# RWKV-7 branch of a hybrid block on one Trainium2 core: token-major tiles by identity products of array parts, in a task of their own, and U and V in a tile per pair

## The chip, the core and the metric

The kernel runs on one core of one Trainium2 chip. A core has five engines that are used here: TensorE (PE, with its weight loads shown as PEld), VectorE (DVE), ScalarE (ACT), GpSimd (POOL) and SyncE (SP), which issues nearly all transfers. Each engine runs its own instructions in their order and waits on semaphores for the others. The metric is the device time of one execution in microseconds. The kernel before takes 2975.77 us, the median of three runs (2969.96 to 2988.65).

## What is computed

A block of two layers maps a latent stream of 256 tokens and a context of 256 tokens, 1024 channels wide, to the latent stream. In each layer a normed input goes through one wide projection into three branches, which are gated and summed, and then through a gated feed-forward part (FFN):

```
p  = rms_norm(x) modulated @ w_in            # columns: mLSTM | RG-LRU | RWKV-7 ("rw") | merge gates
y  = sig(g_ml)*(mlstm(p) @ out_ml) + sig(g_lru)*(rglru(p) @ out_lru) + sig(g_rw)*(rwkv7(p) @ out_rw)
x += gate1 * (y @ w_out);   x += gate2 * swiglu(rms_norm(x) modulated)

# rwkv7, 16 heads of 64, forward and backward over context, then over the latent tokens
kap = k*k_k / norm(k*k_k);  w = exp(-c*sigmoid(decay));  a = sigmoid(iclr);  kt = k*(1+(a-1)*k_a)
def step(S, (r, w, k, v, kap, kapa)):        # per head, state S is 64 x 64
    S = S*w - (S@kap) kapa^T + v k^T
    return S, S@r
out = (layernorm(y)*ln_w + ln_b + sum(r*(kt_f+kt_b)*r_k)*v) * gate
```

## The kernel before

Arrays lie with channels on the partitions and tokens along the free axis. Products in full precision are made of three reduced ones (a high and a low part of weights and input), so a weight block goes from DMA to a cast on ACT (`whi`), a subtraction on DVE (`wlo`) and three matmuls on PE.

The change lies in the RWKV part, which the kernel works out in chunks of 32 tokens. Its work comes in **units**, u = 0 to 7: four groups of two pairs of heads, each once for the context (even u) and once for the latent tokens (odd u). A unit goes through these functions:

- `rw_prep`: the norm of k (from L783), decay and rate from low-rank products (`low`, `wtanh`, `decay`), the scaled arrays (`rows`), and then `chunks` (L759 to 780): products of all 8 chunks of a direction into two PSUM banks of the tag `sm`, masked by DVE into `Am` (L772), and sent to memory for the solve (L778). Behind that stands the **token stage** (L829 to 888): POOL scales `bks` (L830), and k-side and v-side tiles must be brought from channel-major to token-major form, as weights and inputs of the chain. `tokens` (L848) transposes four blocks of 128x128 into one PSUM bank (L852). `quads` (L840) copies the four quarters of that bank to their places with four copies (L845), those of the forward direction on ACT, those of the backward one on DVE. Four banks give `bkT`. Two give `UV`, after two ACT copies that order v by chunk (L876). Between them stands the product for the bonus term `bv` (L869).
- `rw_solve`: 30 pairs of POOL instructions (L930, L932) invert a small triangular system per chunk. Its input N comes from memory (L924), its result goes to memory (L937) and back into `Am` (L942), all on SP's queue.
- `rw_chain`: eight steps, one after the other, for the eight chunks of both directions. In each, PE adds the state's part into `xy`, DVE copies it to `xs` (L1001) and scales the state (L1005), PE multiplies it by the solved `Am` into one PSUM tile `u2`, four copies bring that to `UV` (j=1 on ACT, L1028; j=0 on DVE, L1031), PE makes the state's update and the output, and DVE writes the new state `Sn` (L1046, L1048) and the output (L1058, L1060).
- `rw_tail`: layer norm over the head, a transposing product and the gate.

`rw_prep` runs for the eight units one after the other in one task, `rw_chain` in another. Both, the loads (`rw_load`) and the gate product (`rw_gate`) stand beside the **fills** (`products`): the projections of all branches, 1776 matmuls per layer (L258, tile `mm`). `weave` (L296) sets the order when the program is built: it goes through the tasks in their order in a list, the fills last. A task yields what it waits for: an estimated time (`at`, `on`), an event of another task (`until`), or a lock. A task that can go on is preferred, and a fill is put in whenever PE has lately had fewer than 4800 columns of work in a stretch of estimated time. So every edit of costs or tasks changes where the fills stand.

Behind this stretch stand `ml_gates`, and then `ml_head` and `lru` for four groups (the mLSTM and RG-LRU branches). `gates()` makes the merge-gate products (576 matmuls per layer, L415, loaded by SP in pieces of 512 KB), of which some are put between the heads, and the rest behind them. Then comes the merge (L1486), the output projection and the FFN (L415). The compiler's scheduler orders these sections, and may move their instructions up into the RWKV stretch where that has room.

## Time and profile before

| | kernel before |
| --- | --- |
| median of three runs | 2975.77 us (2969.96 to 2988.65) |
| the profiled execution | 2990.54 us, span 2988.8 us |
| PE busy | 2663.0 us, 89% |
| PEld busy | 2037.4 us, 68% |
| DVE busy | 1877.0 us, 63% |
| ACT busy | 1260.8 us, 42% |
| POOL busy | 794.4 us, 27% |
| mean granted clock of PE | 0.953 |

The profile is one execution, so its times stand against its own 2990.54 us and not against the median. Busy shares are means over stages with different limits. The table alone says that PE is busy for most of the span. The waits of a stage say what an engine stood still for, and the chain of waits is followed back from the last instruction.

### The profile page before, as it was taken

The numbers are of one execution on the slowest core, as the hardware profiler recorded it, in microseconds if no ns is written. First come the engines' busy times: TensorE is split into PE (matmuls) and PEld (weight loads), VectorE is DVE, ScalarE is ACT, GpSimd is POOL, SyncE is SP. The second block draws the span as 40 slices with busy tenths as digits, with TensorE's granted clock in tenths as the row PEclk, the third lists the DMA queues.
The fourth block names the chain that finished last, engine by engine and source line by source line (L and its number), as shares of the span: only waits on it lengthen the run. The fifth ranks groups of instructions, "written<-read, shape, count | busy, mean of one in ns | idle before, by whom it ended". The sixth has DMA issues, their size and how long they took to land.

```text
span 2988.8 us, 64157 instructions
## 1 busy us (share of the span) xinstructions
PE 2663.0 (89%) x25800; PEld 2037.4 (68%) x25800; DVE 1877.0 (63%) x3962; ACT 1260.8 (42%) x2575; POOL 794.4 (27%) x1231
## 2 busy tenths in 40 slices
PE   7988888888989899999999989888888777769998
PEld 4766666666645676777777877666666666349898
DVE  5687777767478624553333367767676856767564
ACT  4443333333257532343222355343444434655553
POOL 1055554546112100020000011554555540100000
PEclk9999999999999999999999999999999988779999
DMA  6443233333353457654554445433334335227454
GB/s 223 164 136 102 87 103 101 93 104 96 108 185 122 152 174 228 213 203 155 167 167 142 128 130 168 130 110 114 110 110 118 106 107 183 80 86 245 154 183 143
DMA packets 242281, 420.59 MB, mean 141 GB/s; under 512 B 86048, under 2 KB 133408, under 8 KB 241984
## 3 DMA queue, kind: packets, MB, share of 16 engines
q1 hardware_dynamic: 240688, 415.39, 44.7%
q8 instruction: 202, 3.31, 0.5%
q10 hardware_dynamic: 1296, 1.10, 0.1%
q14 instruction: 95, 0.78, 0.1%
HBM read 348.75 MB, written 66.62 MB: 139 GB/s over the span
## 4 chain that ended last, share of the span: by engine, by line
PE 43%; DVE 12%; DMA 4%; ACT 4%; issue 3%; POOL 2%; SPq 0%; POOLq 0%; DVEq 0%; ACTq 0%
PE mm L415 22%; PE mm L1486 8%; PE mm L258 4%; DMA wraw<-in_wA_dram 2%; DVE wlo L463 1%; PE xy L1143 1%; DMA yraw<-ysc 1%; PE sm L1324 1%; PE sm L258 1%; PE u L258 1%; DVE UV L1031 1%; PE xy L258 1%; ACT whi L460 1%; PE sc L258 1%; ACT UV L1028 1%
## 5 line engine op out<-in xcount | busy, mean ns | idle before, releaser
L258 PE MATMUL mm<-hl,whi 128*128 128x512 f32 (+1 forms) x1184 | 461.7, 390 | 17.0 <-DVE stage L539 10.6
L258 PE MATMUL mm<-hh,wlo 128*128 128x512 f32 (+1 forms) x1184 | 463.0, 391 | 7.5 <-DVE wlo L463 7.4
L258 PE MATMUL mm<-hh,whi 128*128 128x512 f32 (+1 forms) x1184 | 460.8, 389 | 0.0
L373 DVE TENSOR_TENSOR wlo<-wraw,whi 128x512 fp32r<-128x512 f32 (+1 forms) x310 | 217.0, 702 | 281.9 <-ACT whi L372 279.1
L415 PE MATMUL mm<-hl,whi 128*128 128x512 f32 (+1 forms) x1056 | 367.5, 348 | 6.4 <-ACT whi L372 4.2
L415 PE MATMUL mm<-hh,wlo 128*128 128x512 f32 (+1 forms) x1056 | 363.2, 345 | 5.7 <-DVE wlo L373 5.7
L415 PE MATMUL mm<-hh,whi 128*128 128x512 f32 (+1 forms) x1056 | 362.7, 344 | 0.0
L372 ACT CAST whi<-wraw 128x512 fp32r<-128x512 f32 (+1 forms) x310 | 189.1, 614 | 365.7 <-PE mm L415 246.2
L930 POOL TENSOR_TENSOR et<-N 64x30 f32<-64x30 f32 (+14 forms) x480 | 269.6, 562 | 139.0 <-DMA N<-sc 103.5
L463 DVE TENSOR_TENSOR wlo<-wraw,whi 128x512 fp32r<-128x512 f32 x296 | 228.1, 773 | 117.6 <-ACT whi L460 114.1
L932 POOL TENSOR_TENSOR N<-N,et 64x30 f32<-64x30 f32 (+14 forms) x480 | 291.9, 608 | 36.7
L258 PEld LDWEIGHTS mm<-hl,whi 128*128 128x128 f32 x1184 | 230.5, 195 | 62.3 <-ACT stage L536 8.9
L1172 POOL TENSOR_TENSOR nsq<-nsq,stage 128x256 f32<-128x256 f32 (+1 forms) x28 | 26.1, 933 | 921.4 <-ACT stage L1170 666.2
L258 PEld LDWEIGHTS mm<-hh,wlo 128*128 128x128 f32 x1184 | 229.7, 194 | 54.1 <-DVE wlo L463 12.7
L258 PEld LDWEIGHTS mm<-hh,whi 128*128 128x128 f32 x1184 | 229.7, 194 | 41.7 <-issue 1.9
L460 ACT CAST whi<-wraw 128x512 fp32r<-128x512 f32 x296 | 179.4, 616 | 145.6 <-DMA wraw<-in_wA_dram 100.9
L372 ACT CAST whi<-wx 128x512 fp32r<-128x512 f32 x212 | 128.7, 609 | 260.9 <-PE mm L415 165.0
L373 DVE TENSOR_TENSOR wlo<-wx,whi 128x512 fp32r<-128x512 f32 x212 | 144.6, 683 | 146.3 <-ACT whi L372 144.5
L415 PEld LDWEIGHTS mm<-hl,whi 128*128 128x128 f32 x1056 | 202.0, 191 | 50.7 <-ACT whi L372 20.3
L415 PEld LDWEIGHTS mm<-hh,wlo 128*128 128x128 f32 x1056 | 202.0, 191 | 37.1 <-DVE wlo L373 6.7
L1028 ACT COPY UV<-u 32x128 f32<-32x128 f32 x256 | 65.6, 256 | 371.8 <-DVE UV L1031 371.0
L415 PEld LDWEIGHTS mm<-hh,whi 128*128 128x128 f32 x1056 | 202.1, 191 | 22.1 <-issue 1.0
(324 smaller groups left out, 5502.8 us busy)
## 6 DMA issues: line engine op xcount, KB each, us to landing
wraw<-in_wA_dram SPq DMA_DIRECT2D x275, 512.0 KB, 3.8
wx<-in_wA_dram SPq DMA_DIRECT2D x81, 512.0 KB, 3.5
wx<-in_wM_dram SPq DMA_DIRECT2D x55, 512.0 KB, 4.6
wraw<-in_wM_dram SPq DMA_DIRECT2D x41, 512.0 KB, 4.2
mld<-stage SPq DMA_DIRECT2D x48, 256.0 KB, 2.2
wraw<-in_wB_dram SPq DMA_DIRECT2D x23, 512.0 KB, 3.5
pd<-stage SPq DMA_DIRECT2D x40, 256.0 KB, 2.1
ax<-in_aux_dram SPq DMA_DIRECT2D x32, 256.0 KB, 4.0
```

Of the source, the lines that this page charges most:

```text
L258: self.nc.tensor.matmul(out, lhsT, rhs, start=start, stop=stop)
L372: self.nc.scalar.copy(hi[i], x[i])
L373: self.nc.vector.tensor_tensor(out=lo[i], in0=x[i], in1=hi[i].bitcast(F32), op=ALU.subtract)
L415: self.nc.tensor.matmul(ps, x[k], y[:, koff + k, t0:t0 + n], start=start and i == 0, stop=stop and i == 3 * nk - 1)
L460: self.nc.scalar.copy(hi, x)
L463: self.nc.vector.tensor_tensor(out=lo, in0=x, in1=hi.bitcast(F32), op=ALU.subtract)
L930: G.tensor_tensor(out=tv, in0=N[:, 0:i, i:i + 1].broadcast_to([64, i, w]), in1=N[:, i:i + 1, i + 1:32].broadcast_to([64, i, w]), op=ALU.mult)
L932: G.tensor_tensor(out=N[:, 0:i, i + 1:32], in0=N[:, 0:i, i + 1:32], in1=tv, op=ALU.subtract)
L1028: SC.copy(UV[b, j, :, i], us[b, j])
L1031: V.tensor_copy(UV[b, j, :, i], us[b, j])
L1143: nc.tensor.matmul(ps[32 * q:32 * q + 32], self.cp[:, k], w[:, 256 * q:256 * q + 256], start=k == 0, stop=k == KC - 1)
L1486: self.nc.tensor.matmul(ps, x[k], y[k][:, t0:t1], start=i == 0, stop=i == 3 * KC - 1)
```

## The change

The token stage leaves `rw_prep` and becomes a task, `rw_tok`, spawned beside the solve. The next unit's `rw_prep` begins at once, and waits for the end of this task only before its own `rows` (until "prep", u-1). In it the transposes are replaced by products of 64-row parts of the arrays with a 64x64 part of the identity, written where they belong. So a whole bank can be copied at once, by ACT: two products' groups with two banks each for `bkT`, and two groups with one bank each for U and V, which is copied twice (once per pair). Only the backward direction of v is still reordered first. U and V lie in two tiles, `UV0` and `UV1`, one per pair j; the gate's scratch tiles that shared the tag are split likewise. Two DVE steps, the +1 of `th` and the scaling of `kt`, go to ACT. The two `sm` banks are guarded by a lock, some estimated costs change, and a tail waits for the one before it before it is spawned. From here on some line numbers differ: the UV copies of the chain are L1052 (ACT) and L1055 (DVE) in the changed kernel.

```diff
@@ rw_prep: decay
-            V.tensor_scalar(th, th, 1.0, None, ALU.add)
+            self.locks.discard("sm")
+            SC.activation(out=th, in_=th, func=AF.Identity, bias=self.one)
...
-            V.tensor_scalar(kt, at, self.hka[:, p:p + 1], self.omka[:, p:p + 1], ALU.mult, ALU.add)
+            SC.activation(out=kt, in_=at, func=AF.Identity, scale=self.hka[:, p:p + 1], bias=self.omka[:, p:p + 1])
@@ rw_prep: before the first rows
+                if u:
+                    yield ("until", ("prep", l, u - 1))
+                if yo:
+                    bp = re.tile([128, 2, S], F32, name="bp")
+                yield ("lock", "sm")
@@ rw_prep: end
+        yield ("spawn", self.rw_solve(l, u, Am, sc1))
+        yield ("spawn", self.rw_tok(l, u, ctx_out, bks, bp, v, dict(kr=kr, Am=Am, PL=PL)))
+
+    def rw_tok(self, l, u, ctx_out, bks, bp, v, unit):
...
         for j in range(2):
             G.tensor_tensor(out=bks[j], in0=bks[j], in1=PL[:, j].broadcast_to([128, 2, 8, 64]), op=ALU.mult)
-            t = self.op("G", 1855)
-        yield ("spawn", self.rw_solve(l, u, Am, sc1))
+            t = self.op("G", 1904, self.free["V"])
+        vr = self.tmp([128, 8, 2, 32], "kt")
+        SC.copy(vr[:, ::-1, :, ::-1].rearrange("p c j t -> p j c t"), v.rearrange("p j (c t) -> p j c t", t=CH))
...
-        def tokens(x):
-            ps = self.sm([128, 4, 128])
-            for m in range(4):
-                nc.tensor.transpose(ps[:, m], x[:, 128 * m:128 * m + 128], self.ident)
-            return ps
-        for j in range(2):
-            for d in range(2):
-                ps = tokens(bks[j][:, d].rearrange("p c t -> p (c t)"))
-                yield ("pe", 440, 512)
-                yield from quads("SV"[d], lambda hd, p: bkT[64 * (hd ^ j):64 * (hd ^ j) + 64, j, d, p::2], ps)
+        UV = [rl.tile([128, 2, 8, 64], F32, name=f"UV{j}", bufs=2) for j in range(2)]
+        for d in range(2):
+            yield ("lock", "sm")
+            ps = self.sm([128, 8, 64])
+            for c in range(8):
+                for hd, j in HJ:
+                    b = 64 * (hd ^ j) + 32 * j
+                    x = vr[R[hd], c, j] if d else v[R[hd], j, CH * c:CH * c + CH]
+                    self.mmul(ps[b:b + 32, c], x, self.ident[R[hd], R[hd]])
+            yield self.took()
+            for j in range(2):
+                SC.copy(UV[j][:, d], ps)
...
+        for d in range(2):
+            yield ("lock", "sm")
+            pss = [self.sm([128, 8, 64]) for _ in range(2)]
+            for c in range(8):
+                for j in range(2):
+                    for hd in range(2):
+                        o = 64 * (hd ^ j)
+                        self.mmul(pss[j][o:o + 64, c], bks[j][R[hd], d, c], self.ident[R[hd], R[hd]], quads=True)
+            yield self.took()
+            for j in range(2):
+                SC.copy(bkT[:, j, d], pss[j])
@@ rw_chain
                 if j:
-                    SC.copy(UV[b, j, :, i], us[b, j])
+                    SC.copy(UV[j][b, :, i], us[b, j])
                 else:
-                    V.tensor_copy(UV[b, j, :, i], us[b, j])
+                    V.tensor_copy(UV[j][b, :, i], us[b, j])
...
         if yo:
+            if n > (0 if ctx_out else 1):
+                yield ("until", ("tail", l, n - 1 if ctx_out else n - 2))
             yield ("spawn", self.rw_tail(l, n, Y, u["bv"], emit))
```

What this does to the order of the instructions is seen at three places. A row is one instruction, or several alike in a row, as the engine gets them: line, operation, output tile<-input tile, shape, and how many.

**First place: PE, the token stage of unit 0 of layer 0.** `mm` are fills, `sm` the banks of the token stage, `bk` the scaled arrays `bks`, `cst` the identity. In the kernel before the four banks for `bkT` stand between fills as four transposes each:

```order
L852 MATMUL sm<-cst,bk 128x128 x4
L258 MATMUL mm<-hh,whi 128x512
L852 MATMUL sm<-cst,bk 128x128 x4
L258 MATMUL mm<-hh,wlo 128x512
L258 MATMUL mm<-hl,whi 128x512
L258 MATMUL mm<-hh,whi 128x512
L852 MATMUL sm<-cst,bk 128x128 x4
L258 MATMUL mm<-hh,wlo 128x512
L852 MATMUL sm<-cst,bk 128x128 x4
```

In the changed kernel the bonus product (`bp`) stands ahead of the two groups for `bkT`, and the next unit's norm (`tmp`) and first low-rank product (`dd`) follow five fills behind:

```order
L258 MATMUL sm<-bp,cst 64x512 x2
L258 MATMUL sm<-cst,bk 64x64 x32
L258 MATMUL mm<-hl,whi 128x512
L258 MATMUL mm<-hh,whi 128x512
L258 MATMUL sm<-cst,bk 64x64 x32
L258 MATMUL mm<-hh,wlo 128x512
L258 MATMUL mm<-hl,whi 128x512
L258 MATMUL mm<-hh,whi 128x512
L258 MATMUL mm<-hh,wlo 128x512
L258 MATMUL sm<-cst,tmp 128x2 x4
L258 MATMUL sm<-dd_455,ah 128x256
```

Sixteen transposes in four banks have become 64 products in two groups of two banks, and the groups for U and V (two of 32 products, 32x64) have moved ahead of them.

**Second place: ACT, among the chain steps of a unit of layer 0.** The waits that an instruction carries stand behind it in brackets. In the kernel before the chain's copies of U (L1028) stand between the token copies (L845) and the start of the next unit (L783):

```order
L845 COPY UV<-sm 32x4x64 [waits PE_49]
L845 COPY UV<-sm 32x4x64 x6
L1028 COPY UV<-u_4666 32x2x64 [waits DVE_49] x2
L845 COPY UV<-sm 32x4x64
L460 CAST whi<-wraw 128x512 [waits Activation_49]
L783 ACTIVATE tmp<-kr_4332,vecs 128x256 [waits DMAHW4_49,Activation_49]
L783 ACTIVATE tmp<-kr_4332,vecs 128x256
L1028 COPY UV<-u_4779 32x2x64 [waits DVE_49] x2
```

In the changed kernel they stand between casts and the next unit's decay (L696 to L707):

```order
L1052 COPY UV_3178<-u_4928 32x2x64 [waits DVE_49] x2
L460 CAST whi<-wraw 128x512
L678 CAST ah<-ax 128x512 [waits DMAHW7_49]
L696 ACTIVATE th<-sm,dvec 128x256 [waits PE_49,Activation_49]
L696 ACTIVATE th<-sm,dvec 128x256
L704 ACTIVATE at<-sm,dvec 128x256 [waits PE_49]
L704 ACTIVATE at<-sm,dvec 128x256
L707 ACTIVATE th<-th,one 128x512 [waits Activation_49]
L1052 COPY UV_3178<-u_5036 32x2x64 [waits DVE_49] x2
```

The copies now write a tile of their own (`UV_3178`), and each of them carries a wait on DVE as before; what stands between two steps is another part of another unit.

**Third place: PE, the last chain step of layer 1.** `xy<-Sn` and `u<-xs` are the chain's products. In the kernel before only merge-gate products (L415) are left to stand between them:

```order
L258 MATMUL xy<-Sn,kr 32x64 x8
L258 MATMUL sc<-Sn,kr 32x64 x8
L415 MATMUL mm<-hl,whi 128x256
L258 MATMUL u_26809<-xs,Am 32x64 x8
L415 MATMUL mm<-hh,whi 128x256
L415 MATMUL mm<-hh,wlo 128x256
L415 MATMUL mm<-hl,whi 128x256
```

In the changed kernel fills stand there:

```order
L258 MATMUL xy<-Sn,kr 32x64 x8
L258 MATMUL sc<-Sn,kr 32x64 x8
L258 MATMUL mm<-hh,wlo 128x512
L258 MATMUL mm<-hl,whi 128x256
L258 MATMUL mm<-hh,whi 128x256
L258 MATMUL u_27899<-xs,Am 32x64 x8
L258 MATMUL mm<-hh,wlo 128x256
L258 MATMUL mm<-hl,whi 128x256
```

Of the 576 gate products of layer 1, 567 stood ahead of the mLSTM section before. In the changed kernel none does: 195 stand inside that section and 381 behind it.

## Rows read from the trace of the kernel before

**Rows 1.** Windows: length; busy us (count) PE, PEld, DVE, ACT, POOL; clock, DMA, GB/s
```profile
50.00:825.00 775.00, 687.69 (x9482) 503.82 (x9481) 549.41 (x1220) 296.19 (x673) 338.91 (x523) 0.96 0.38 111
825.00:1018.00 193.00, 168.08 (x646) 96.61 (x644) 155.47 (x368) 132.32 (x234) 43.20 (x72) 0.97 0.42 135
1751.00:2360.00 609.00, 528.93 (x6854) 412.56 (x6852) 438.36 (x934) 263.21 (x605) 288.63 (x442) 0.95 0.41 122
2360.00:2510.00 150.00, 120.92 (x2108) 103.35 (x2108) 98.00 (x231) 57.95 (x137) 46.50 (x78) 0.92 0.42 127
2510.00:2674.00 164.00, 109.45 (x374) 58.89 (x374) 122.96 (x276) 100.86 (x181) 20.37 (x49) 0.78 0.34 101
```

**Rows 2.** windows, L415 alone, 2360 to 2510: PE, PEld busy, clock, DMA, GB/s
```profile
2360.00:2510.00 150.00, 86.88 (x566) 74.45 (x566) 0.92 0.42 127
```

**Rows 3.** one line's instructions in layer 0: ns least/middle/most, first to last start
```profile
L783 ACT ACTIVATE tmp<-kr,vecs x16: 492/503/506, 105.2 to 658.0; 128x256 f32<-128x256 f32 x16
L1001 DVE COPY xs<-xy x64: 270/291/292, 219.9 to 803.6; 128x128 f32<-128x128 f32 x64
```

**Rows 4.** the same, unit 4: masked products, token copies, next unit's start
```profile
L772 DVE TENSOR_TENSOR Am<-sm,cst x4: 680/686/692, 465.4 to 470.4; 128x512 f32<-128x512 f32 x4
L845 DVE COPY UV<-sm x8: 411/420/429, 491.5 to 496.2; 32x256 f32<-32x256 f32 x8
L783 ACT ACTIVATE tmp<-kr,vecs x2: 492/499/506, 494.4 to 495.3; 128x256 f32<-128x256 f32 x2
```

**Rows 5.** the same, unit 4: solve steps on POOL, then chain steps
```profile
L930 POOL TENSOR_TENSOR et<-N x30: 228/576/890, 477.8 to 528.9; 64x30 f32<-64x30 f32 x2, 64x58 f32<-64x58 f32 x2, 64x84 f32<-64x84 f32 x2, 64x108 f32<-64x108 f32 x2
L1001 DVE COPY xs<-xy x8: 277/289/292, 541.1 to 585.0; 128x128 f32<-128x128 f32 x8
```

**Rows 6.** PE's waits, 50 to 825: waiting tile <- releaser: us, times, longest
```profile
PE u L258 <- ACT UV L1028: 28.8, 40, 2.2
PE u L258 <- DVE xs L1001: 15.4, 9, 4.6
```

**Rows 7.** PE's waits, 1751 to 2490, columns as before
```profile
PE u L258 <- ACT UV L1028: 30.4, 36, 2.9
PE xy L258 <- DVE Sn L1048: 24.7, 14, 14.7
```

**Rows 8.** timeline: start, us, engine, copy [wait <- releaser] in one chain step
```profile
2463.69 0.28 DVE L1031 COPY UV<-u 32x128 f32<-32x128 f32 x1 [0.26 <-PE u L258]
2464.30 0.30 DVE L1031 COPY UV<-u 32x128 f32<-32x128 f32 x1 [0.33 <-ACT UV L1028]
2464.01 0.26 ACT L1028 COPY UV<-u 32x128 f32<-32x128 f32 x1 [2.93 <-DVE UV L1031]
```

**Rows 9.** timeline of PE: one masked product's group, one transposed bank
```profile
701.51 1.16 PE L258 MATMUL sm<-kr,bk 64*64 64x64 f32 x64
477.59 0.60 PE L852 MATMUL sm<-cst,bk 128*128 128x128 f32 x4
```

**Rows 10.** lines by form: out<-in, count, then busy us, mean ns, idle before
```profile
L845 ACT COPY bkT<-sm 64x256 f32<-64x256 f32 x128 | 46.9, 367 | 27.2 <-PE sm L852 25.6
L1244 ACT COPY stage<-mm 128x512 f32<-128x512 f32 x50 | 29.1, 582 | 47.3 <-PE mm L258 47.1
L845 DVE COPY bkT<-sm 64x256 f32<-64x256 f32 x128 | 54.0, 422 | 17.2 <-PE sm L852 15.2
L708 DVE TENSOR_SCALAR th<-th 128x512 f32<-128x512 f32 x32 | 17.9, 558 | 10.0 <-ACT th L698 9.7
```

**Rows 11.** SP queue's waits, whole span: us, times, longest
```profile
SPq L937 <- POOL N L934: 88.7, 15, 17.9
```

**Rows 12.** chain of waits: start, us, what ran
```profile
2791.65 175.99 PE mm L415 x1463
2493.62 1.64 POOL var L1089
2510.61 0.59 DVE W L1367
```

More of the change, by code (lines that the diff above doesn't have):

```diff
@@ L590, in take @@
             yield self.at("V", 335)
[L591 removed]
+            self.gd = self.rl.tile([128, 2, T], F32R, name="gd", tag="UV0", bufs=2)
             self.split(self.gd[:, 0, t0:], self.gd[:, 1, t0:], x[:, t0:])
@@ L606, in rw_gate @@
         yield ("wait", 4500)
-        w = self.rl.tile([128, 2, KC, 128], F32R, name="gw", tag="UV", bufs=2)
+        w = [self.rl.tile([128, KC, 128], F32R, name="gw", tag=x, bufs=2) for x in ("UV0", "UV1")]
         for i in range(2):
-            hi, lo = (w[:, x, 4 * i:4 * i + 4].rearrange("p k c -> p (k c)") for x in range(2))
+            hi, lo = (x[:, 4 * i:4 * i + 4].rearrange("p k c -> p (k c)") for x in w)
             x = raw[:, 512 * i:512 * i + 512]
@@ L670, in rw_prep @@
         PL = rl.tile([128, 2, 2, 8, 1], F32, name="PL", bufs=3)
-        bv = None
-        if yo:
-            bp = re.tile([128, 2, S], F32, name="bp")
+        bp = None
         def ct(x):
@@ L836, in rw_prep @@
             yield ("until", ("chain", l, u - 2))
[L837 to L859 removed]
+        UV = [rl.tile([128, 2, 8, 64], F32, name=f"UV{j}", bufs=2) for j in range(2)]
+        for d in range(2):
+            yield ("lock", "sm")
+            ps = self.sm([128, 8, 64])
[7 more added lines that the diff above has]
+                SC.copy(UV[j][:, d], ps)
+                t1 = self.at("S", 582)
+                if j:
+                    self.locks.discard("sm")
+                yield t1
+        bv = None
         if yo:
@@ L869, in rw_prep @@
             V.tensor_tensor(out=bv, in0=bps, in1=v, op=ALU.mult)
-            yield self.at("V", 602)
-        UV = rl.tile([128, 2, 2, 8, 64], F32, name="UV", bufs=2)
-        vs = []
+            self.locks.discard("sm")
+            yield self.at("V", 691)
+        yield ("at", t + LAT)
+        bkT = rl.tile([128, 2, 2, 8, 64], F32, name="bkT", bufs=2)
         for d in range(2):
-            x = self.tmp([128, 8, 2, 32], "kt" if d else "tmp")
-            SC.copy((x[:, ::-1, :, ::-1] if d else x).rearrange("p c j t -> p j c t"), v.rearrange("p j (c t) -> p j c t", t=CH))
-            vs.append(x)
-            yield self.end("S", 520)
-        for d in range(2):
-            ps = tokens(vs[d].rearrange("p c j t -> p (c j t)"))
-            yield ("pe", 440, 512)
-            for j in range(2):
-                def rows(hd, p):
-                    b = 64 * (hd ^ j) + 32 * j
-                    return UV[b:b + 32, j, d, p::2]
-                yield from quads("SV"[d], rows, ps, slice(32 * j, 32 * j + 32))
-        self.unit[u] = dict(kr=kr, Am=Am, bkT=bkT, PL=PL, UV=UV, bv=bv)
+            yield ("lock", "sm")
+            pss = [self.sm([128, 8, 64]) for _ in range(2)]
[5 more added lines that the diff above has]
+            yield self.took()
+            for j in range(2):
+                SC.copy(bkT[:, j, d], pss[j])
+                t1 = self.at("S", 582)
+                if j:
+                    self.locks.discard("sm")
+                yield t1
+        self.unit[u] = dict(unit, bkT=bkT, UV=UV, bv=bv)
         self.done.add(("prep", l, u))
@@ L986, in tokens @@
                     v = slice(b, b + 32)
-                    self.mmul(x[U(hd, j), d], Am[v, j, d, i, 0:32], UV[v, j, d, i], start=d == 0 or one, stop=one)
+                    self.mmul(x[U(hd, j), d], Am[v, j, d, i, 0:32], UV[j][v, d, i], start=d == 0 or one, stop=one)
             return x
```

36 lines of the change are left out of this document (21 added, 15 removed).

## The prediction

> **What bounds the kernel now.** I read the windows by stage first, then the places of single lines in one RWKV stretch, then the waits of PE, SP and the chain's copies, and last the durations.
>
> The RWKV part runs once in each layer, beside the projections ("fill products", line 258, 1776 of them per layer). In layer 0 it lasts from 50 to about 825 us, and PE is busy for 688 of the 775 us [rows 1]; DVE stands at 549, ACT at 296, POOL at 339. In layer 1 it begins at 1751; the last fill product starts at 2359, but work goes on: between 2360 and 2510 PE is busy for 120.9 us, of which 86.9 belong to the merge-gate products (L415) of the section behind [rows 1, 2]. So 34 us of RWKV work stand behind the last fill. The section behind (mLSTM and RG-LRU) then takes 164 us with PE busy for only 109, at a clock of 0.78 (between the two levels of 1.2 and 2.4 GHz) [rows 1].
>
> What sets the pace inside is the preparation of a unit. The 16 first instructions of the preparations of layer 0 (two in each of eight units) lie between 105.2 and 658.0, so a unit comes every 79 us; the 64 chain steps end at 803.6 [rows 3]. In unit 4 the masked products end at about 471 and the last token copy at 496.2, and only then does unit 5 begin, at 494.4 [rows 4]: 25 of the 79 us are the token stage, which nothing in the next preparation's first part needs. The chain of unit 4 starts only at 541.1, since its solve on POOL runs from 477.8 to 528.9 [rows 5].
>
> **The change, part by part.**
>
> *The token stage as its own task.* The next unit's norm and first product no longer wait for it. I read from the order how far this goes: in layer 0 the last chain step stood behind 1699 of the 1776 fills and now behind 1426; in layer 1 it stood behind all 1776 and 418 gate products, and now behind 1658 fills. Both RWKV stretches therefore become bound by PE's own work, and an earlier chain gains only where PE had stood still.
>
> *Layer 1, from the last fill to the merge* (2359 to 2674, 315 us). The 34 us of RWKV work go in front of the last fill. The next section can start some 4 us behind it: now 17 us pass from the tail's pow at 2493.6 to the first gate scan at 2510.6 [rows 12], and in the new order the tail's product has 73 fills, some 13 us, behind it. Its 164 us stay, plus 8 for 195 gate products that the order now puts into it (195 at 0.12 us, the pace of 1463 such products in 176 us [rows 12], are 23 us; 55 us of PE's time there are free, so I take a third; bounds 0 and 23). The other 381 stand behind it all: 46 us, plus 5 since each 24 of them need a load of 512 KB (bounds 0 and 12), less 6 for the merge's first load, which lies beneath them (bounds 0 and 10). 34 + 4 + 164 + 8 + 46 + 5 - 6 = 255: **60 us less**.
>
> *Products for transposes.* 24 transposes of a unit, six banks of 0.60, become four groups of 32 small products [rows 9]. The nearest row is a group of the masked product, 32 products (64 records) in 1.16 us, the same quadrants. 4 x 1.16 - 6 x 0.60 = +1.04 us a unit, **+17 us** over 16 units. Bounds: 0, if the slots overlap with the fills beside them, and +40, if each of the four changes between whole array and quadrants costs 0.35 us more. The Trainium skill (TensorEngine Tiling (Array Packing), Key Properties) says that changing the tiling mode drains the engine, which speaks against the change; the 1.16 us of the row already hold one such change, so by the rule the sum would be the same.
>
> *Copies of whole banks.* 32 copies of a quarter bank, half of them on DVE at 0.42 us, become eight of 0.58 on ACT alone [rows 10]. With the two element-wise steps that move from DVE to ACT (0.56 each [rows 10], twice a unit each) DVE loses 9.0 us a unit, ACT gains about 1. Neither is the bound (549 and 296 of 775 [rows 1]), so I take only 5 us for it (bounds 0 and 20): **-5**.
>
> *U and V in two tiles.* In a chain step DVE and ACT copy alternately, 0.28, 0.26 and again 0.30: ACT starts 0.32 us behind DVE, and DVE 0.29 behind ACT [rows 8]; PE waits 28.8 and 30.4 us for the last of them [rows 6, 7]. The split might let them run side by side. But all four read one PSUM tile, and in the built order both copies still carry a wait on the other engine (second place of the order above). I take nothing. The Trainium skill (PSUM — Partial Sum Buffer, PSUM bank collisions raise a hardware error) has two engines in one bank and quadrant as the error and different quadrants as free; the four copies lie in four quadrants, so by that rule they could overlap. The trace shows them alternating all the same; what their overlap would give is in the third rival.
>
> *Chain steps further apart.* A chain of layer 0 had 442 fills between its first and last steps (all eight units) and now has 562, 27% more. PE's waits inside a step shrink where more stands in between. They are 28.8 + 15.4 [rows 6] and 30.4 + 24.7 [rows 7], less the longest, 14.7, which I count with layer 1's end: 84.6. If the same sum of waits is covered by 1.27 times the work, a fifth goes: **-18** (bounds 0 and -60).
>
> *The solve, nearer to its use.* From the masked products' end to the chain's start a unit had 145 fills in the middle of layer 0 and now 125, some 5 us less, while the solve keeps its 51 us on POOL [rows 5]. SP waited 88.7 us in 15 units for POOL's result [rows 11], 5.9 each, and the weight loads queue behind it. It will wait about 11. Of such waits little reached PE so far; I take **+10** (bounds 0 and +90, if all 16 units pay the 5 us in full).
>
> *Layer 0's next section.* The gate scans and the first convolutions now stand among the last fills; PE idles 25 us in this section now [rows 1]. **-5** (bounds +10 and -20).
>
> Sum: -60 + 17 - 5 - 18 + 10 - 5 = **-61 us**. The profiled execution took 2990.5 us, so it would take about 2930; the median of the three runs shown, 2975.8, lies 15 us lower, so I predict **2915 us** against it.
>
> **The rivals.**
>
> 1. *More is gained.* PE's waits inside the chain steps mostly go (84.6 us instead of 18), since more work stands between, or since the copies run side by side after all. For it: 76 waits on the last copy of 0.8 us each, a small piece of work covers them. Against it: the order still alternates. -61 - 50 gives about 2865. Chance 0.17.
>
> 2. *The gate products come back in full.* They hid beneath layer 1's chains; behind them they cost their 23 and 57 us (loads included), and ACT's whole-bank copies hold chain copies up: 128 bank copies, if half of them stand ahead of one that is due, are 37 us. For it: [rows 2] shows how much was hidden, and ACT executes in order. The Trainium skill (TensorEngine Tiling, PSUM Bottleneck) advises both engines for emptying PSUM, as the kernel before does. Against it: ACT is free for six tenths of the time. -61 + 15 + 12 (loads and the merge's first load) and some of the 37 gives -20 or so: 2955. Chance 0.18.
>
> 3. *Slower: the solve becomes the bound.* POOL needs 51 us of solve, 4 of scaling and some 5 of roots in each unit, and units now come every 67 to 70 us. If SP's wait grows by 5 us a unit and the fills behind it stand still for it, 16 units lose 80 us and the time is about 2990; it turns into a loss from 4 us a unit on, beyond the 10 that the sum holds. At 8 us a unit it is 3030. For it: SP already waits up to 17.9 us at a time [rows 11]. Against it: the loads run two blocks ahead. Chance 0.07.
>
> **How the numbers follow.** The forecast has 0.58. A measurement of this kernel can tell about 1%, 30 us, from no change. Faster by more than that (under 2946): the forecast, the first rival and a little of the second, less the forecast's upper edge: 0.78. Within 1%: most of the second rival and a part of the third: 0.17. Slower: 0.05. The range reaches from the first rival's 2860 to 2965, past the second; the third lies beyond it. The forecast's own range is 2885 to 2945.
>
> **What would show it.** Right: the unit pace of layer 0 falls from 79 to about 67 to 70 us, the last chain step of layer 0 comes near 730 instead of 804 while the last fill stays within 25 us of 825; in layer 1 the last chain step comes before the last fill, the last fill near 2390, and a block of some 380 L415 products of about 46 us stands ahead of the merge. ACT's copy of U would still be released by DVE. Wrong: PE waits for the chain's rows or scaled factors to come back from POOL, SP's wait on POOL well above 180 us, layer 1's section behind above 185 us, or small products whose group of 32 takes clearly more than 1.2 us.

## The result, and the profile after

The changed kernel takes **3015.7 us** (median of 4 runs, 3013.8 to 3017.6) against 2980.7 us of the kernel before beside it: ratio 1.0121, 95% interval 1.0095 to 1.0148. It is slower by 1.2%, where 2% faster was forecast. Its profiled execution took 3013.8 us, 23 us more than that of before.

PE's busy time was 2663.0 us before. The engines' row on the page (busy us, share, instructions) is now:

```profile
PE 2701.0 (90%) x29512; PEld 2061.9 (68%) x29512; DVE 1766.9 (59%) x3642; ACT 1264.9 (42%) x2496; POOL 808.2 (27%) x1231
```

DVE lost 110 us and the kernel is slower all the same; PE works 38 us more. To see where, I cut the span at four points: first fill of a layer, its first merge product, and the end. Columns as in [rows 1]; "waits" below are a stretch's length less PE's busy time in it. First before (layer 0 to its merge, layer 1 to its merge, the rest), then after (with layer 1 also cut at its last fill):

```profile
50.00:1104.00 1054.00, 941.21 (x10483) 669.57 (x10482) 733.29 (x1628) 458.03 (x958) 384.35 (x596) 0.96 0.40 123
1752.00:2663.00 911.00, 754.38 (x9313) 570.39 (x9311) 650.09 (x1428) 418.75 (x919) 354.47 (x566) 0.92 0.40 120
2663.00:2989.00 326.00, 298.87 (x2376) 293.15 (x2376) 202.11 (x374) 158.32 (x302) 15.38 (x20) 0.93 0.55 176
```

```profile
52.00:1125.00 1073.00, 953.97 (x12336) 675.88 (x12335) 678.57 (x1468) 460.14 (x918) 387.07 (x596) 0.98 0.39 121
1772.00:2489.00 717.00, 611.68 (x10236) 468.99 (x10235) 450.11 (x957) 286.92 (x629) 343.64 (x519) 0.92 0.38 108
2489.00:2704.00 215.00, 178.05 (x937) 127.85 (x938) 155.41 (x334) 138.62 (x264) 23.58 (x49) 0.89 0.51 158
1772.00:2704.00 932.00, 789.73 (x11173) 596.85 (x11173) 605.52 (x1290) 425.54 (x892) 367.23 (x568) 0.91 0.41 119
2704.00:3012.00 308.00, 291.27 (x2378) 287.54 (x2376) 191.65 (x354) 153.57 (x290) 13.49 (x18) 0.97 0.58 182
```

Layer 0 is 19 us longer (PE's work +13, its waits 113 to 119), layer 1 is 21 us longer (work +35, waits 157 to 142), and behind the last merge starts 18 us are won. The units did get faster, as the lines that answer to [rows 3] show (starts of preparation, chain steps of layer 0, chain steps of layer 1):

```profile
L784 ACT ACTIVATE tmp<-kr,vecs x16: 493/517/528, 107.0 to 621.7; 128x256 f32<-128x256 f32 x16
L1025 DVE COPY xs<-xy x64: 272/290/293, 226.9 to 772.4; 128x128 f32<-128x128 f32 x64
L1025 DVE COPY xs<-xy x64: 273/291/294, 1943.5 to 2465.7; 128x128 f32<-128x128 f32 x64
```

A unit comes every 73 us instead of 79, and the last step of layer 0 starts at 772 instead of 804. But the fills end at 858 instead of 825. PE's waits in the chain, which answer to [rows 6] and [rows 7], did not shrink (layer 0, then layer 1):

```profile
PE u L258 <- ACT UV L1052: 37.5, 45, 2.8
PE xy L258 <- DVE Sn L1072: 15.0, 19, 2.1
PE u L258 <- DVE xs L1025: 10.4, 12, 1.8
...
PE u L258 <- ACT UV L1052: 42.9, 40, 2.7
PE xy L258 <- DVE Sn L1072: 15.5, 18, 2.5
```

The waits for the copies of U rose from 28.8 and 30.4 to 37.5 and 42.9 us. And the small products cost more than four times 1.16 us a unit. Rows by form (busy us, mean ns, then PE idle before them), before and after:

```profile
L852 PE MATMUL sm<-cst,bk 128*128 128x128 f32 x256 | 41.4, 286 | 9.1 <-DVE bkT L845 6.1 <-issue 2.6 <-ACT bkT L845 0.2
L852 PE MATMUL sm<-cst,kt 128*128 128x128 f32 x64 | 10.5, 289 | 0.0
L852 PE MATMUL sm<-cst,tmp 128*128 128x128 f32 x64 | 10.1, 281 | 1.2 <-ACT tmp L876 1.2
```

```profile
L258 PE MATMUL sm<-cst,bk 64*64 64x64 f32 x2048 | 48.8, 232 | 15.2 <-DVE bv L892 5.4 <-ACT th L696 4.0 <-issue 3.6
L258 PE MATMUL sm<-cst,kt 64*32 64x64 f32 x1024 | 18.7, 218 | 3.5 <-issue 3.5
L258 PE MATMUL sm<-cst,v 64*32 64x64 f32 x1024 | 18.5, 223 | 0.0
```

Busy time alone goes from 62 to 86 us. Counted in the trace from the first record of each group to the start of the next other product, their place in PE's queue goes from 52 us (96 banks) to 100 us (64 groups, 6.2 us a unit). The timeline shows why the groups for `bkT` are the dear ones (start, us, then idle before them and its releaser; two groups of layer 0):

```profile
331.76 0.91 PE L258 MATMUL sm<-cst,bk 64*64 64x64 f32 x42
334.35 0.57 PE L258 MATMUL sm<-cst,bk 64*64 64x64 f32 x22 [1.68 <-issue]
...
684.18 0.33 PE L258 MATMUL sm<-cst,bk 64*64 64x64 f32 x4
685.13 1.15 PE L258 MATMUL sm<-cst,bk 64*64 64x64 f32 x60 [0.62 <-DVE bv L892]
```

Such a group writes both `sm` banks in turn. In the second one shown, PE stands after the first four records until the second bank is free, which DVE has first to empty of the bonus product, and executes nothing else meanwhile. In the first one it stands in the middle of the group, and the profile names no cause.

### The profile page after: what moved, and what is told of

Read it like the earlier page. It is cut to its first block, busy times and chain, and to the rows that moved or that the text cites. A ratio compares the mean times of both kernels' runs of the same rounds, so it can differ in the third digit from the quotient of the medians.

```text
span 3012.1 us, 71136 instructions
## 1 busy us (share of the span) xinstructions
PE 2701.0 (90%) x29512; PEld 2061.9 (68%) x29512; DVE 1766.9 (59%) x3642; ACT 1264.9 (42%) x2496; POOL 808.2 (27%) x1231
## 5 line engine op out<-in xcount | busy, mean ns | idle before, releaser
L415 PE MATMUL mm<-hh,wlo 128*128 128x512 f32 (+1 forms) x1056 | 361.9, 344 | 18.1 <-DVE wlo L373 18.0
L415 PE MATMUL mm<-hl,whi 128*128 128x512 f32 (+1 forms) x1056 | 366.9, 347 | 7.3 <-ACT whi L372 3.5
L415 PE MATMUL mm<-hh,whi 128*128 128x512 f32 (+1 forms) x1056 | 360.3, 341 | 0.0
L463 DVE TENSOR_TENSOR wlo<-wraw,whi 128x512 fp32r<-128x512 f32 x296 | 236.0, 800 | 135.2 <-ACT whi L460 132.8
L954 POOL TENSOR_TENSOR et<-N 64x30 f32<-64x30 f32 (+14 forms) x480 | 279.0, 581 | 63.8 <-DMA N<-sc 27.6
L415 PEld LDWEIGHTS mm<-hl,whi 128*128 128x128 f32 x1056 | 202.3, 192 | 56.2 <-ACT whi L372 20.5
L415 PEld LDWEIGHTS mm<-hh,wlo 128*128 128x128 f32 x1056 | 202.1, 192 | 47.7 <-DVE wlo L373 21.3
L1052 ACT COPY UV<-u 32x128 f32<-32x128 f32 x256 | 65.6, 256 | 386.3 <-DVE UV L1055 385.6
L415 PEld LDWEIGHTS mm<-hh,whi 128*128 128x128 f32 x1056 | 202.6, 192 | 23.0 <-issue 3.2
```

The costliest lines, as they stand in the source:

```text
L415: self.nc.tensor.matmul(ps, x[k], y[:, koff + k, t0:t0 + n], start=start and i == 0, stop=stop and i == 3 * nk - 1)
L463: self.nc.vector.tensor_tensor(out=lo, in0=x, in1=hi.bitcast(F32), op=ALU.subtract)
L954: G.tensor_tensor(out=tv, in0=N[:, 0:i, i:i + 1].broadcast_to([64, i, w]), in1=N[:, i:i + 1, i + 1:32].broadcast_to([64, i, w]), op=ALU.mult)
L1052: SC.copy(UV[j][b, :, i], us[b, j])
```

## The experiments

Ratios are to the kernel before, run beside each. The expectations name theories by letter. A: the fills stand too thin for the faster units. B: PE's own work grew by the small products. C: the whole-bank copies on ACT hold the chain's copies up. D and O: the task of its own, by its overlap, is what costs. W: PE waits because too little work stands between a chain step's products.

**Means against order.** The first question was whether the products, or the order of the fills, cost the time. `after_transposes` keeps the task, the split tiles and the steps on ACT, and takes transposes and quarter copies again; `before_products` puts the products and the whole-bank copies into the preparation of the kernel before, with one tile for U and V and the two steps on DVE.

```diff
# after_transposes, in rw_tok, for bkT (U and V likewise)
-                        self.mmul(pss[j][o:o + 64, c], bks[j][R[hd], d, c], self.ident[R[hd], R[hd]], quads=True)
...
-                SC.copy(bkT[:, j, d], pss[j])
...
+                ps = blocks(bks[j][:, d].rearrange("p c t -> p (c t)"))
...
+                yield from quads("SV"[d], lambda hd, p: bkT[64 * (hd ^ j):64 * (hd ^ j) + 64, j, d, p::2], ps)
# before_products, in rw_prep: the same lines the other way round
```

(`blocks` makes the four transposes of the kernel before.)

> The changed kernel, task and split tiles kept, but with the old means: transposes of 128x128 blocks and quarter-bank copies on ACT and DVE in place of the small products and the whole-bank copies. Theory B: PE's work falls by the 35 us that the small products cost more (40.6 + 40.8 less 23.8 + 22.5), and the time by about as much: 2975 to 2990. Theory A: the price lies in the fills' placing, so at most half of it comes back by the less work (3000 or more), unless the new order closes the gaps too: with this kernel 1519 fills stand before the last step of layer 0. Theory C: the chain's waits for its UV copies fall from 80 us to 60 or less, time 2990 to 3000.

> The kernel before with only the means exchanged: small products and whole-bank copies on ACT inside the preparation, no task of its own, one UV tile, DVE keeps its two element-wise steps. Theory B (PE's work grows with the small products, 81.4 us against 46.9 in all, and that is the whole loss): PE works 34 us longer, time 3000 to 3015, which is where the changed kernel stands, and the task of its own then brings nothing. If the copies of whole banks shorten the preparation so much that they pay for the products (the term of 5 us of the prediction, bound 20): 2985 to 2995. Rival D (the task of its own is what costs): at most 10 us above the kernel before.

Measured: 2982.2 us, 1.0017 (0.9998 to 1.0036), and 2983.0 us, 1.0025 (1.0006 to 1.0044). So each half alone loses under half a per cent, and the two together lose 1.2%. With the transposes 33 us come back, as theory B said: PE's work in the two layers falls from 1744 to 1694 us. The same products inside the preparation cost some 7 us (13 at the interval's upper end), where theory B expected 3000 to 3015 us. PE does work longer there, 1727 us where the kernel before has 1696, but it waits less, 246 us for 269. So the products' work is there in both, and is not the loss by itself. And the task of its own, without the products, brings nothing: the forecast's main gain was wrong by itself.

**How dense the fills stand.** `after_dense52`, `after_dense60` and `before_dense52` change one line, `transposes_dense52` the same in `after_transposes`.

```diff
-COLS = [4800, 4800]
+COLS = [5200, 5200]     # or 6000
```

> The changed kernel with the planner's column target raised from 4800 to 5200 in both layers; nothing else differs. By the built order, the last chain step then has 1654 fills before it in layer 0 (1426 in the changed kernel) and all 1776 in layer 1 (1658). Theory A (the time was lost because the faster unit tasks were paired with the old target: the fills are too thin while the chains run, PE waits about 205 us in the two stretches, and 350 and 118 fills run alone behind the last step): waits in the two stretches fall by 25 to 50 us, time 2965 to 2990. Theory B (PE's own work grew: the small products take 40.6 and 40.8 us per layer where the transposes took 23.8 and 22.5, and no placing of fills gives that back): within 8 us of the changed kernel's 3015.7. Theory C (ACT's whole-bank copies hold the chain's copies up): also little, above 3005.

> The same with a target of 6000: all fills stand before the last chain step in both layers, with 98 and 322 gate products as well. Theory A: the optimum is passed, since the chain then ends behind the fills, but still better than the changed kernel, 2975 to 3000. Theories B and C: within 10 us of the run with 5200.

> The control: the kernel before with 5200 instead of 4800. Theory A: before, the target was already matched to the unit pace (1699 of 1776 fills before the last step of layer 0), so nothing is gained: 2970 to 2995. If a denser target helps the kernel before as much as the changed one (25 us and more), the target is a fault of both and Theory A explains no difference between them.

> The same kernel with transposes, and the planner's column target at 5200 instead of 4800. In the changed kernel this took 22 us off (3015.7 to 2993.9). Theory A (the faster unit tasks want denser fills): again 15 to 25 us less, 2958 to 2968, which would be below the kernel before. If the gain there came only from its small products' lying in layer 1's end: within 6 us of 2982.

Measured: 2993.9 (1.0065, 1.0045 to 1.0085), 3009.4 (1.0102, 1.0067 to 1.0137), 2980.3 (1.0027, 1.0004 to 1.0050) and 2962.9 us (0.9965, 0.9946 to 0.9985). A target of 5200 takes some 20 us off both kernels with the task of its own (15 to 17 by the ratios) and nothing off the kernel before. That is theory A by its direction. Its ranges were missed: 2993.9 lies 4 us above, and 3009.4 with 6000 lies 9 us above. PE's waits while the fills last fell by 23 us (205.7 to 182.8), where 25 to 50 were expected. It does not give the whole loss back.

**What a single chain step has to cover.** Counted in the built order, 3.2 fills (in layer 1 with gate products) stand on the mean of layer 0 between a step's product for U and the product that reads the copies (6.2 in layer 1), and in the changed kernel 4.0 (6.3). A copy of U is done 1.4 to 1.9 us (medians) behind that product's end, a fill takes 0.23 us, so many steps are covered too little in either. I call the work between the two products the step's cover. Four kernels allow 0.5 us more there in the planner, and three of them also at the new state:

```diff
-WAIT = [0, 0, 0]
+WAIT = [0, 500, 0]      # *_wait;   [0, 500, 500] in *_wait_state
```

> The changed kernel with transposes and quarter-bank copies (as the run before it of that name, 2982 us), and in the planner 0.5 us more allowed between a step's product for U and the product that reads the copies. By the built order 5.67 fills stand there on the mean of layer 0 instead of 4.47, and 9.13 instead of 6.95 in layer 1; the last chain step keeps its place. Theory W (PE's waits of about 200 us in the two stretches come from each step's own few fills, whatever the pace of the units, and that is why the earlier units bring nothing): PE's waits for the copies (44.9 and 40.7 us there) fall by a third to a half, time 2950 to 2970. Rival: the waits only move to the steps' other two places (xs and the state): within 6 us of 2982.

> The changed kernel (small products and all), with 0.5 us more allowed in the planner between a step's product for U and the product that reads the copies. By the order 5.95 fills stand there on the mean in layer 0 instead of 4.00, and 8.90 instead of 6.30 in layer 1, and in layer 1 the last chain step moves from behind 1658 fills to behind all 1776. Theory W (PE's waits in the chain are set by the few fills of each step): PE's chain waits in the two stretches fall from 147 to 110 us or less, and layer 1's low clock in that stretch (0.92) rises to 0.94 or more: 2985 to 2995, 25 us less. What is then left against the same with transposes (2964.6) is the products' own price: 20 to 35 us. If the whole-bank copies on ACT hold the chain (Theory C), the waits do not fall by more fills: above 3005.

> The control: the kernel before with the same 0.5 us. By the order 5.43 fills instead of 3.23 in layer 0 and 7.45 instead of 6.20 in layer 1. If the waits of a step are common to both kernels, it gains as much as the kernel with transposes and the task of its own (18 us): 2950 to 2962, and the task of its own brings nothing at all. If the kernel before has no room for longer chain steps, since its chain ends with its fills: 2968 to 2990.

> The kernel before with small products and whole-bank copies inside the preparation (2983.0 without more), and with 0.5 us more ahead of the product that reads the U copies. Against 2940.0 with transposes it tells the price of the products where the steps' waits are covered: theory B says 20 to 35 us (PE works 34 us longer), 2960 to 2975, which would be the changed kernel's 2970.0 with the same wait and leave nothing for the task of its own. If the products stay as cheap as without the wait (9 us): 2945 to 2955, and the overlap costs the other 15 to 25.

> The changed kernel with 0.5 us more allowed in two places of each step: ahead of the product that reads the U copies (that alone gave 2970.0) and ahead of the next step's product with the new state Sn. With the first alone, PE's longest waits stood at Sn (28.9 us in layer 0, 32.2 in layer 1). Theory W: these fall to 15 or less each, 2945 to 2958. If the chain then ends too late, or the waits move on to xs: 2963 to 2978.

> The control, the kernel before with both. With the first alone it took 2940.0 and its waits at Sn were 18.8 and 13.7 us. Theory W: 10 to 15 us less at most, 2925 to 2938. If its chains, which end behind the fills in layer 1, are what sets the end: no gain or a loss, 2938 to 2955.

> Transposes in the task of its own, with 0.5 us more at both places of a step (the changed kernel with both took 2948.9, the kernel before 2946.4). Theory B (products) on top of theory W: with the waits covered the 34 us of PE work come back nearly in full, since PE is the bound: 2915 to 2930, which would beat every kernel so far. If the transposes' quarter copies on DVE hold Sn and xs up (with the wait for U alone this kernel took 2964.6 and the kernel before 2940.0): 2935 to 2960.

> Transposes in the task of its own, with both: 0.5 us more per step and the target of 5200. Each alone gave 2964.6 and 2962.9 against 2982.2. If they close different waits the gains add: 2943 to 2952, about 1% below the kernel before. If both cover the same waits: 2955 to 2965.

| ratio to before | as it was | 0.5 us at U | at U and the state |
| --- | --- | --- | --- |
| the kernel before | 1 | 0.9897 (0.9871 to 0.9923), 2940.0 us | 0.9886 (0.9869 to 0.9904), 2946.4 us |
| the changed kernel | 1.0121 | 0.9976 (0.9953 to 0.9999), 2970.0 us | 0.9891 (0.9870 to 0.9912), 2948.9 us |
| with transposes | 1.0017 | 0.9973 (0.9955 to 0.9991), 2964.6 us | 0.9950 (0.9934 to 0.9966), 2964.1 us |
| before, with products | 1.0025 | 1.0032 (1.0019 to 1.0044), 2987.9 us | not run |

With transposes and both the denser target and 0.5 us at U: 2970.3 us (0.9985, 0.9969 to 1.0001); the two gains do not add. One number in the planner moves the changed kernel by 46 us, a second one by 67 us in all, more than any of its parts, and with both allowances it stands level with the kernel before under the same two. PE's waits in layer 0 show a part of how: in `after_wait` those for the copies fall to a third and those for the state rise, and in `after_wait_state` those for the state fall and those for `xs` rise.

```profile
PE xy L258 <- DVE Sn L1072: 28.9, 20, 2.9
PE u L258 <- ACT UV L1052: 11.9, 14, 1.8
PE u L258 <- DVE xs L1025: 6.6, 8, 1.5
```

```profile
PE xy L258 <- DVE Sn L1072: 15.7, 16, 2.8
PE u L258 <- DVE xs L1025: 14.8, 18, 2.1
PE u L258 <- ACT UV L1052: 12.0, 15, 2.2
```

In `before_wait` the waits for U in layer 0 are down to 7.1 us from 28.8:

```profile
PE xy L258 <- DVE Sn L1048: 18.8, 21, 2.2
PE u L258 <- DVE xs L1001: 11.9, 9, 4.1
PE u L258 <- ACT UV L1028: 7.1, 13, 1.2
```

Five expectations failed. The control was to gain some 18 us and gained 1%, the best time of all. The changed kernel with the first allowance was to take 2985 to 2995 us and took 2970.0. Transposes with the allowance and the denser target took 5 us more than even the range for gains that don't add. The kernel before with products gained nothing: its waits for U fell from 49.0 to 19.8 us in layer 0, but only from 42.7 to 36.1 in layer 1, where its other waits grew. And transposes under both allowances were to be the fastest by 34 us of PE's work and are 15 us slower than the products. There the shared banks are a part of the price: in layer 0 the preparation's next products wait for the quarter copies to leave a bank (PE's waits):

```profile
PE sm L258 <- ACT UV L866: 7.2, 5, 2.1
PE sm L872 <- DVE bkT L866: 4.9, 6, 1.3
```

PE's work in the two layers is 1694 us there and 1708 in `after_wait_state`, its waits 252 and 225. The waits shown are 12 of these 27 us. That whole-bank copies pay where the chain's steps are covered is read from this one pair of kernels; none changes them alone.

**The overlap, the copies, the tiles.** Three kernels undo one part each of the changed one.

```diff
# after_serial, in rw_prep ahead of the norm
+        if u:
+            yield ("until", ("prep", l, u - 1))
# after_split_copies, both places
-                SC.copy(bkT[:, j, d], pss[j])
...
+                (V.tensor_copy if j else SC.copy)(bkT[:, j, d], pss[j])
...
# after_one_uv (the gate's scratch tiles likewise)
-        UV = [rl.tile([128, 2, 8, 64], F32, name=f"UV{j}", bufs=2) for j in range(2)]
+        UVt = rl.tile([128, 2, 2, 8, 64], F32, name="UV", bufs=2)
+        UV = [UVt[:, j] for j in range(2)]
```

> The changed kernel with one part undone: the next unit's preparation begins only when the token task of the unit before is done, so nothing overlaps; products, whole-bank copies, split tiles and steps on ACT stay. By the order, 1507 fills stand before the last chain step of layer 0 (1426 in the changed kernel), and in layer 1 all 1776 and 82 gate products (1658 and none). Theory O (the overlap itself costs: the next unit's steps on DVE and ACT get ahead of the chain's, and the fills get too thin): back near the kernel before with the same products, 2980 to 2990, 25 to 35 us less. If the overlap is harmless and the other parts (locks, split tiles, steps on ACT) cost: 3008 to 3025.

> The changed kernel with its whole-bank copies shared: those of pair 0 stay on ACT, those of pair 1 go to DVE. Theory C (the eight copies of 0.58 us on ACT stand ahead of the chain's copies there): the chain's waits fall, 2995 to 3008. Theory B and W (products and fills): within 8 us of 3015.7, apart from what the changed order of fills does (1549 instead of 1426 before the last step of layer 0, 1734 instead of 1658 in layer 1), which Theory A puts at 10 us or so.

> The changed kernel with U and V in one tile again; the order of instructions stays. My theory (DVE and ACT copy alternately since all four read one PSUM tile): no change, 3010 to 3020, and the copies alternate in both. If the split tiles had let them run side by side: the chain's waits grow by 128 times 0.3 us, part of it seen: 3025 to 3050.

Measured: 2994.8 (1.0060, 1.0038 to 1.0082), 3006.6 (1.0120, 1.0094 to 1.0146) and 3018.9 us (1.0152, 1.0116 to 1.0187). Taking the overlap away makes the changed kernel 21 us faster: theory O by its direction, short of its 25 to 35 us. Its mechanism isn't shown: PE waits for U there as long as before, 42.0 and 41.8 us in the two layers. Sharing the copies changes nothing that can be told from the ratio. Its median is 9 us lower and lies in theory C's range, but the waits for U, which were to fall, are longer in layer 0 than the 37.5:

```profile
PE u L258 <- ACT UV L1052: 42.8, 50, 2.9
```

So the whole-bank copies are not what holds the chain, and theory C falls. The tiles do nothing that can be told.

**The trace of before once more.**

> The kernel before once more, unchanged, for a second trace of it, to see which terms are steady: PE's work in both stretches within 5 us of the first trace, its waits too; the wait of 14.7 us at Sn in layer 1 (SP blocked by POOL's solve while a gate load stands behind) either again at the same place within 5 us, or not at all. The time between 2962 and 2992.

2966.7 us. The waits are steady:

```profile
PE u L258 <- ACT UV L1028: 29.5, 39, 2.8
PE xy L258 <- DVE Sn L1048: 24.4, 15, 14.7
```

(layer 1's RWKV stretch.) The 14.7 us stall stands there again to the tenth. PE's work is not steady to 5 us: 934 and 744 in the two layers, against 941 and 754, and the layers last 1041 and 900 us against 1054 and 911. So a difference of some 13 us in one layer of a single trace says nothing. Against this second trace the changed kernel's layers are 32 and 32 us longer, against the first 19 and 21, in both cases mostly by PE's work. `after_one_uv`, with the changed kernel's order, serves as a second trace of that. The windows of the other traces, cut at the same points, say the same (us, both layers together up to the merge; then what follows the last merge's start):

| kernel | PE's work | PE's waits | behind |
| --- | --- | --- | --- |
| the kernel before, two traces | 1696, 1678 | 269, 263 | 326, 323 |
| the changed kernel, `after_one_uv` | 1744, 1738 | 261, 261 | 308, 308 |
| `after_transposes` | 1694 | 272 | 316 |
| `before_products` | 1727 | 246 | 316 |
| `after_serial` | 1729 | 247 | 313 |
| `before_wait` | 1674 | 247 | 323 |
| `after_wait` | 1732 | 233 | 311 |
| `after_wait_state` | 1708 | 225 | 314 |
| `transposes_wait_state` | 1694 | 252 | 317 |

The changed kernel waits no longer than the kernel before; it works 42 to 66 us longer. In this table all kernels with the products work 1708 us and more, all with transposes 1696 and less. Of the 72 us that the two allowances take off its layers, 36 are waits and 36 are work, by the same instructions.

## Why the prediction was wrong

- **The step that failed first: "Both RWKV stretches become bound by PE's own work."** They were bound by PE's work plus its waits, and I had too little of both: a unit came sooner, but PE's waits in the chain steps did not follow the units' pace, and its work grew. From layer 1's last fill I moved 34 us of RWKV work in front of the fill and left behind the 29 us that PE waited in the same 150 us (150 less 120.9, [rows 1]). By my terms the last fill starts 651 us behind the first (608 + 34 + half of the 17); it came at 716. Of these 65 us, 25 are waits (105 in the stretch, where I had some 80), and 40 are work, for which the next three points give what the traces show.
- **"Chain steps further apart: -18" had the wrong sign for U.** The chain's waits for U went up by 21 us. It was not that less stood between a step's product and its reader: in layer 0 it was more (4.0 fills for 3.2), in layer 1 the same. The copies came later. I had looked at the work that covers them and not at DVE's queue, in which the first of the four stands behind the steps of a unit's preparation. On the mean of 64 steps it started 0.64 us behind the product's end in layer 0 and 0.80 in layer 1, where it was 0.44 and 0.58 before (0.65 and 0.83, 0.41 and 0.56 in the second traces). That is 13 or 14 us a layer, and PE's waits for the copies rose by 9 and 13. One such step, with PE's wait behind it (PE's product had ended at 407.0):

```profile
408.19 0.69 DVE L724 TENSOR_TENSOR kt<-kt,kr 128x512 f32<-128x512 f32 x1 [1.19 <-ACT kt L722]
409.40 0.68 DVE L735 SCALAR_TENSOR_TENSOR at<-at,kap 128x512 f32<-128x512 f32 x1
410.11 0.28 DVE L1055 COPY UV<-u 32x128 f32<-32x128 f32 x1
411.35 0.61 PE L258 MATMUL u<-UV,bkT 64*64 64x64 f32 x16 [2.42 <-ACT UV L1052]
```

  `after_wait` shows that more cover takes these waits away, not that too little of it brought them.
- **Products: +17, and it was about 48** (52 to 100 us of PE's queue), beyond the bound of 40. The mechanism was right, and the size off at two points: a transposed bank keeps PE's queue 0.54 us on the mean and not 0.60, and the groups for `bkT` take 1.9, since they want two banks at once. Those for U and V take 1.2 on the mean (1.03 at the median), near the row's 1.16. That row was one of the quick ones: the 32 masked groups of the trace of before, which also use two banks, take 1.44 us on the mean from start to next start, ten of them more than 1.5, and by 1.44 the same sum gives some 40 us. My sign of being wrong, groups clearly above 1.2 us, came true. In what the kernel pays it is no fixed price: against transposes, in the task of its own, the products cost 34 us, 5, and then save 15, as the planner's allowance grows.
- **The fills themselves: no term.** In layer 1 they were to take what they took before. All the 256-wide fills lie there (before and after):

```profile
L258 PE MATMUL mm<-hl,whi 128*128 128x256 f32 x264 | 76.5, 290 | 2.3 <-DVE stage L539 2.1 <-ACT whi L460 0.3
```

```profile
L258 PE MATMUL mm<-hl,whi 128*128 128x256 f32 x264 | 82.2, 311 | 4.0 <-DVE stage L539 3.7 <-ACT whi L460 0.3
```

  Each of three times 264 lasts some 20 ns longer. These durations overlap; counted from start to start, 53 of the 256-wide ones took 0.21 or 0.22 us in place of 0.12 before, the pace of the clock's lower level, and 148 after. That is some 9 us (74 and 128 in the second traces: 5). The granted clock of the stretch went from 0.95 and 0.92 ([rows 1]) to 0.92, while that of the section behind rose from 0.78 to 0.89. Whether the one is the price of the other isn't shown; over the whole layer it is 0.92 before and 0.91 after.
- **Layer 1's section behind: right in the sum, by luck.** By the terms 4 + 153 (to the first merge product) + 8 + 46 + 5 it would start the merge 216 us behind the last fill; it took 215, with all 576 gate products in it. But the block of 381 of them took 60 us and not 51, and what stands ahead of it 155 and not 165:

```profile
2488.40:2643.80 155.40, 126.48 (x559) 78.74 (x557) 121.09 (x279) 104.34 (x196) 21.52 (x47) 0.88 0.42 131
2643.80:2704.00 60.20, 51.87 (x383) 49.20 (x383) 34.82 (x59) 34.87 (x70) 2.06 (x2) 0.91 0.73 227
```

  What follows the merge's start is 18 us shorter (15 by the second trace), where I had 6 for its first load. PE's waits there for `ylo`, 14.6 us before, are gone behind the block of gate products:

```profile
PE mm L1486 <- DVE ylo L373: 14.6, 4, 7.1
```

- **Copies of whole banks: -5**, not seen. DVE lost 110 us in all, 6.9 a unit where 9.0 were reckoned. It was not the bound, but what stands in its queue ahead of a chain copy counts, as said above. For the two steps that moved to ACT it now waits 47 us in all (10 for the one it had from ACT before), of which 1 us a layer lies right ahead of a chain copy. No kernel undoes these two steps alone; with them and transposes, `after_transposes` is level with the kernel before. **U and V in two tiles: nothing**, right, shown by `after_one_uv`.
- **The solve: +10**, not seen. SP's wait for POOL's result fell to 47.2 us (12 times) from the 88.7 of [rows 11], where I had it double; rival 3 falls with it. **Layer 0's next section: -5**, right in sign: 279 us (275 in the second trace) from last fill to merge before, 268 now.
- Of what was to show it, the last chain step before the last fill in layer 1 and the copy of U released by DVE came true; the unit pace (73 for 67 to 70), layer 0's last step (773 for 730) and last fill (857, 32 us late where 25 were allowed) and layer 1's last fill (2488 for 2390) did not. No rival was it: the gates came back in the sum as forecast and no further, the copies on ACT that the second rival named hold nothing up (`after_split_copies`), and the solve did not become the bound.

What stays open is why each arrangement moves the time by another amount: the same products cost from -15 to +48 us and the same allowance from -46 to +5, since every edit places some 1776 fills per layer anew. Shown is that the products add to PE's work wherever they stand, that the changed kernel's waits didn't shrink enough to pay for it, that 0.5 us more in the planner shortens the waits for U in both layers of all four kernels, and that the changed kernel equals the one before when both have both allowances. The kernel before with either allowance and the changed one with both are 1.0 to 1.1% under the kernel before, and can't be told apart.

## What to carry to other kernels

Where one engine's queue carries both a chain of dependent steps and the work that is to hide them, look first at how much work stands between each product and its reader, against the time that its copies take, and at what stands ahead of these copies in their own engine's queue; the pace of the whole chain says nothing of either. When work is moved in front of a mark, move the waits with it: a stretch's length is busy time plus waits, and only a wait that something covers is won. And a change of means shifts the planner's order, so compare it at more than one setting of the planner before it gets a price.

## What the runs showed of the hardware

A group of 32 small products (64 records) into two PSUM banks stood still after its first four records in 23 of the 32 groups, 0.4 to 1.0 us, with PE's whole queue behind it, while 32 into one bank took 1.03 us at the median. In two groups PE stood 1.7 and 1.9 us in mid-group with no wait that the profile names (331.76 above is one); instruction fetches rose from 202 packets to 231 with the 1664 added products, but that these are the cause wasn't tried. On ACT, the two moved element-wise steps took 0.72 and 0.80 us, where DVE took 0.56 and 0.58.
